# Hybrid encoder trunk: score products padded to 128 rows, and other prices in the planning clock

## The chip, the cores and the metric

The kernel runs on one core of a Trainium2 chip, in one launch. The metric is the device time of that launch in microseconds. TensorE (PE) multiplies, VectorE (DVE) and ScalarE (ACT) do the element-wise work, GpSimd (POOL) a few small operations, and SyncE (SP) issues the loads.

## The reference

Two layers of a block with four parallel branches, for 256 tokens of width 1024, all in float32. What matters here are the scores: per layer, two attentions and a retention of four heads of width 64 each.

```python
h = rms_norm(x, norm_mix_g)
rq, rk, rv, rg, pv, nq, nk, nv, mq = jnp.split(h @ w_in, 9, axis=-1)
...
sc = jnp.einsum('bhrnqd,bhrnwkd->bhrnqwk', qg, kg).astype(jnp.float32) * (d ** -0.5) + bias[None]
...
sc = jnp.einsum('bhsd,bhmd->bhsm', q, mk).astype(jnp.float32) * (q.shape[-1] ** -0.5)
...
scores = jnp.einsum('bhncd,bhnmd->bhncm', qc, kc) * d_intra[None, :, None].astype(dt)
...
x = x + merged @ w_out
a, g = jnp.split(rms_norm(x, norm_ffn_g) @ w_ffn_in, 2, axis=-1)
return x + (jax.nn.silu(a) * g) @ w_ffn_out
```

## The kernel before

The tokens form two tiles of 128 (tile 0, tile 1). The weights pass as slots of [128, 1024] in a fixed order: SyncE loads a slot into one of four `raw` buffers, ScalarE rounds it into one of ten `whi` buffers, VectorE makes the rest `wlo = raw - whi`. The left operands are split in the same way (`hhi`, `hlo` for the normalised activations, `bhi`, `blo` for the branches and the FFN's hidden part), and each product of 128 x 512 is three products: hi by hi, hi by lo, lo by hi. A slot gives six of them for each tile. The results gather in the PSUM banks `A` (two for each tile) and `B`; the banks `C` take transposes and what the branches need.

The order of all queues is written at build time by a planner. `Clock` holds an estimate of when each engine gets to what it was given: `Engine` passes on every call and enters it with a price from `Clock.cost`, `Clock.enter` adds waits for operands. The main loop emits a slot of products for one tile, and between groups of three products `background` lets go on those chains of small work (norms, heads, attention, gates, the FFN's hidden part) whose operands should be there by this clock, and `pump` hands out splits of weights. So a price changes no result, and shifts where small work stands between the products.

The scores of a head are made by `scores`. `to_heads` lays out `LS`: for head parity i, hi of the 64 rows of the head on its own partitions, and lo on the other 64. `RS` has hi of the right side on both halves, `RL` lo of it on the head's own 64. So the first product (`rs,ls`, 128 rows) gives hi by hi plus lo by hi, and the second (`rl,ls`, 64 rows) hi by lo. An attention calls it four times in a row, for two heads and both tiles, in two rounds; the retention calls it twice for each head. `log_sigmoid` makes the logarithms of the decays once, in layer 0, in scratch tiles of its own; `rgb` is a gain that is loaded later.

The names in the rows: `A<-whi,hhi` is a product of a rounded slot with a rounded activation, `C<-ident_gain,w` a transpose of a head's or the hidden part's tile `w`, `mem<-in_pool_a` the load of the pooling matrices into the buffers that held the memory tokens. L59 is the line that passes on every recorded call, so nearly all rows have it.

Of the kernel before, what the change touches and what calls it, by code (L numbers as in the profile page):

```python
# [9 lines left out]
F32 = mybir.dt.float32  # L10
# [25 lines left out]
WARM = 6.6  # L36
WINDOW = (6, 4, 1.5, 0.4)
# [5 lines left out]
class Engine:  # L43
    """An engine of nc whose instructions are also entered in the clock."""
# [4 lines left out]
    def __getattr__(self, op):  # L49
        f = getattr(self.real, op)  # L50

        def call(*args, **kw):
            outs = [kw[k] for k in ("out", "accum_out") if kw.get(k) is not None]
            ins = [v for k, v in kw.items() if k not in ("out", "accum_out")]
            rest = list(args)
            if "out" not in kw:
                outs.append(rest.pop(0))
            self.clock.enter(self.name, op, outs, [v for v in ins + rest if isinstance(v, bass.AP)], kw)
            return f(*args, **kw)  # L59

        return call


class Clock:
    """An estimate in microseconds of when each engine gets to what has been given to it:
    the small work is handed out when its operands should be there, so that no queue waits on it."""
# [3 lines left out]
    def __init__(self):  # L70
        self.at = dict.fromkeys(("PE", "ACT", "DVE", "POOL", "SP", "DMA"), 0.6)
        self.reads, self.writes = {}, {}
        self.mark = 0.0
        self.column = None

# [4 lines left out]
    def cost(self, eng, op, outs, ins, kw):  # L80
        n = max([x.free_size() for x in outs[-1:] + ins[:1]])
        if eng == "PE":
            o = outs[0]
            n = o.free_size() * (2 if self.now < WARM else 1)
            if op == "transpose":
                return n * 0.84e-3
            if ins[0].dtype == F32R:
                return n * 0.416e-3 + 0.003
            half = o.partition_size() == HD and o.base_partition()
            if o.partition_size() == HD:  # L90
                pair, self.column = self.column, None if half else n
                if half and pair == n:
                    return 0.02
            return max(n, 128) * 1.67e-3
        if eng == "ACT":
            return 0.1 + n * 0.83e-3 + 0.1 * (kw.get("accum_out") is not None) + 0.04 * isinstance(kw.get("scale"), bass.AP)
        if eng == "POOL":
            return 0.3 + 0.17 * n
        if op in ("tensor_copy", "tensor_scalar", "tensor_scalar_mul", "tensor_scalar_add", "memset"):
            return 0.07 + n * 0.55e-3  # L100
        return 0.07 + n * 1.05e-3 + 0.05 * (op == "scalar_tensor_tensor")
# [18 lines left out]
    def enter(self, eng, op, outs, ins, kw):  # L120
        ins = [x for x in ins if x.space != bass.MemoryType.DRAM]
        outs = [x for x in outs if x.space != bass.MemoryType.DRAM]
        skip = "PE" if eng == "PE" else None
        t = max([self.last(self.writes, x) + self.LATENCY for x in ins]
                + [self.last(self.reads, x, eng) + self.LATENCY for x in ins if x.space == bass.MemoryType.PSUM]
                + [max(self.last(self.writes, x, skip), self.last(self.reads, x, skip)) + self.LATENCY for x in outs] + [self.at[eng]])
        if op == "dma_start":
            self.at[eng] = t + 0.48
            t = max(self.at["DMA"], t + 1.1) + (outs + ins)[0].nbytes() / 360e3
            self.at["DMA"] = t  # L130
            end = t + 0.9
        else:
            end = self.at[eng] = t + self.cost(eng, op, outs, ins, kw)
        for x in ins:
            self.note(self.reads, x, end, eng)
        for x in outs:
            self.note(self.writes, x, end, eng)
        self.mark = max(self.mark, end)
# [9 lines left out]
def tile_encoder(ctx: ExitStack, tc: tile.TileContext, a: dict, out: bass.AP):  # L148
# [29 lines left out]
    RL = st([P, 2, S], F32R, "rl")  # L178
# [108 lines left out]
    def pump():  # L287
        """split weights when the engines have caught up, the sooner the fewer slots are ready"""
        window = WINDOW[max(0, min(state["lo"] - items[min(pos[0], len(items) - 1)]["j"], len(WINDOW) - 1))]
        if state["urgent"]:  # L290
            window = min(window, 0.8)
        for _ in range(2):
            j = state["lo"]
            if j < state["hi"] and soon(clock.at["DVE"], window) and soon(clock.last(clock.writes, WHI[j % NS])):
                split_lo()
            j = state["hi"]
            if (j < min(n_slots, state["free"] + NS, state["lo"] + NR) and soon(clock.at["ACT"], window)
                    and soon(clock.last(clock.writes, RAW[j % NR]))
                    and soon(max(clock.last(clock.reads, w[j % NS]) for w in (WHI, WLO)))):
                split_hi()  # L300
# [31 lines left out]
    def start(gen, *reads):  # L332
        """reads: PSUM banks that gen still reads, until it calls done()"""
        hold(*reads)
        chains.append([clock.now, gen])

    def until(step):
        """a chain goes on after what it has just given out (None), that much later (a number), or at a time"""
        return step[0] if isinstance(step, tuple) else clock.mark + (step or 0)

    def background():
        """let every chain go on whose last instructions should be through"""
# [39 lines left out]
    def scale_rows(out, in_, col):  # L382
        """out = in_ * col, on the engine that is free sooner"""
# [6 lines left out]
    def hi_lo(hi, lo, ps, bank, flag):  # L390
        """hi now, lo when hi is there, which ends the hold on bank"""
# [14 lines left out]
    def half_norm(src, t, c, act, gain, flag, bank, pre=None):  # L406
        """Half c of src (token-major) transposed, times gain (there a column), and split.
        What follows the products with it scales by one over the RMS (rms_chain)."""
# [22 lines left out]
    def rms_chain(src, rs, junk, flag, after=()):  # L431
        """rs = one over the RMS of each row of src"""
# [11 lines left out]
    def norm(t, flag, gain, rs, pre):  # L444
        """both halves of the norm of X[t]"""
# [7 lines left out]
    def head_norm(ps, dst, g, scale=None):  # L453
        """dst = ps (times scale, by row) scaled to unit RMS in groups of 64, g of them."""
# [78 lines left out]
    def to_heads(left, right, gains):  # L533
        """Token-major [tok, 256], both, to heads with the token in the free dimension, split for scores left^T right:
        LS has hi of a head on its 64 partitions and lo on the others, RS hi on both, and RL lo."""
# [31 lines left out]
        for i in range(2):  # L567
            lo(RL[own[i]], C[1], gains[1], i, RS[own[i], i])
# [3 lines left out]
    def scores(out, h, tok):  # L572
        """the scores of head h, for the tokens tok of left, with all of right"""
        r, i = h // 2, h % 2
        own = slice(i * HD, (i + 1) * HD)
        nc.tensor.matmul(out, LS[:, i, r, tok], RS[:, i, r, :], start=True, stop=False)
        nc.tensor.matmul(out, LS[own, i, r, tok], RL[own, r, :], start=False, stop=True)

    def attention(l, v, branch, bias):
        """softmax(q k + bias) v for four heads, two at a time, to BHI/BLO[branch]."""  # L580
# [122 lines left out]
    def decay_chain(l):  # L703
        """exp(|i - j| log gamma): the lesser of d lg_fwd and -d lg_bwd, both of which are at most 0 on their side"""
# [17 lines left out]
    def prefetch_chain(l):  # L722
        """parameters, and what comes in once the layer's norms are through"""
# [33 lines left out]
    def log_sigmoid():  # L757
        """lg = log sigmoid of the 16 decays: min(x, 0) - log1p(exp(-|x|))."""
        t0, t1, t2 = (st([P, 16], F32, f"ls{i}") for i in range(3))
# [26 lines left out]
    def add(n_js, act, bank, nk, n=512, first=True, last=True, req=None, end=None, lag=1):  # L786
        """bank(t) (+)= act of tile t @ the weights of the next n_js slots; nk k-tiles.
        req: what has to be there; end(t): what follows; lag: slots by which tile 0 may lead here."""
# [53 lines left out]
    def hid_chain(l, j, t, ps):  # L842
        """silu(a) * g, token-major"""
# [25 lines left out]
    def layer(l):  # L869
# [23 lines left out]
        for n, br in enumerate(BRANCHES):  # L893
            for blk in range(2):
# [3 lines left out]
                # the gates of the first branch lie around the memory's product  # L898
# [49 lines left out]
    def ready(t):  # L948
        """when the next slot of tile t can be taken"""
# [34 lines left out]
    def warm(*aps):  # L984
        """products of zeros, which keep TensorE at its full clock until aps are there"""
# [9 lines left out]
    with tc.manual_schedule():  # L995
        nc.vector.memset(W[0][:, 0:P], 0.0)
        nc.vector.memset(mhalf, -0.5)
        def load_x(t, c):
# [118 lines left out]
```

## Time and profile before

| | us |
|---|---|
| three runs | 849.38, 851.39, 854.74 |
| their median | 851.39 |
| the profiled execution, span from first to last instruction | 850.4 |
| TensorE busy in it | 840.0 |
| VectorE busy | 553.3 |
| ScalarE busy | 469.6 |

The profiled execution has its span alone; no other time is recorded around it, and the span lies between the fastest and the slowest run. TensorE's granted clock is 0.998 of full speed over the span. Products overlap: each row of a product has a start and a duration, and what a product costs is read from the start of one to the start of the next. An engine's row with [us <-releaser] stood idle that long before it.

### The profile page before, as it was taken

What the parts mean: (1) busy time and instruction counts of PE and PEld (TensorE: products, weight loads), DVE (VectorE), ACT (ScalarE), POOL (GpSimd) and SP (SyncE); (2) the same over time, 40 slices, a digit from 0 to 9 for tenths busy, and PEclk for the clock granted to TensorE, in tenths of its full rate; (3) what the DMA queues carried; (4) which work ended last, traced back from release to release, by engine and by line L of the source; (5) the groups of instructions that cost most, each with busy time, mean ns of one, the idle gap of its engine ahead of it and who ended that gap; (6) DMA issues with size and microseconds to landing.
All of it is one profiled execution on the core that took longest, in us unless ns stands there. A gap on an engine that the chain in (4) does not pass through costs nothing.

```text
span 850.4 us, 10796 instructions
## 1 busy us (share of the span) xinstructions
PE 840.0 (99%) x3934; PEld 678.6 (80%) x3934; DVE 553.3 (65%) x807; ACT 469.6 (55%) x722; POOL 28.6 (3%) x30
## 2 busy tenths in 40 slices
PE   8999999999999999999999999999999999999998
PEld 7887777778887888888888877777788878888886
DVE  5898776665667656555568778567665775665541
ACT  7867867444556444444469676664454654444430
POOL 0300100000000000000012001000000000000000
PEclk9999999999999999999999999999999999999999
DMA  8946764454558666665363567345554675656611
GB/s 267 315 131 202 246 201 132 131 191 160 191 169 259 188 196 187 186 188 186 96 218 121 173 216 250 134 124 182 165 170 131 190 252 183 190 181 192 193 53 50
DMA packets 103749, 152.86 MB, mean 180 GB/s; under 512 B 6416, under 2 KB 55312, under 8 KB 103696
## 3 DMA queue, kind: packets, MB, share of 16 engines
q1 hardware_dynamic: 103696, 152.17, 56.3%
q8 instruction: 31, 0.51, 0.2%
q14 instruction: 22, 0.18, 0.1%
HBM read 151.10 MB, written 1.05 MB: 179 GB/s over the span
## 4 chain that ended last, share of the span: by engine, by line
PE 94%; DMA 3%; DVE 1%; ACT 1%; SPq 0%; issue 0%; DVEq 0%; ACTq 0%
PE A L59 62%; PE B L59 27%; PE C L59 5%; DMA raw<-in_w_ffn_out 2%; DMA mem<-in_pool_a 1%; DVE wlo L59 1%; DMA x<-in_x 1%; ACT whi L59 1%; DVE w L59 0%; SPq L59 0%; DVE x L59 0%; DVEq L1113 0%; ACTq L59 0%
## 5 line engine op out<-in xcount | busy, mean ns | idle before, releaser
L59 DVE TENSOR_TENSOR wlo<-raw,whi 128x1024 fp32r<-128x1024 f32 (+1 forms) x275 | 329.9, 1211 | 183.6 <-ACT whi L59 182.7
L59 ACT CAST whi<-raw 128x1024 fp32r<-128x1024 f32 x272 | 284.3, 1051 | 221.2 <-PE A L59 102.1
L59 PE MATMUL A<-whi,hhi 128*128 128x512 f32 (+1 forms) x544 | 215.6, 396 | 0.1
L59 PE MATMUL A<-whi,hlo 128*128 128x512 f32 (+1 forms) x544 | 209.4, 385 | 0.0
L59 PE MATMUL A<-wlo,hhi 128*128 128x512 f32 (+1 forms) x544 | 209.0, 384 | 0.0
L59 PEld LDWEIGHTS A<-whi,hhi 128*128 128x128 f32 x544 | 102.4, 188 | 24.1 <-issue 5.5
L59 PEld LDWEIGHTS A<-whi,hlo 128*128 128x128 f32 x544 | 102.4, 188 | 21.2 <-DVE hlo L59 0.5
L59 PEld LDWEIGHTS A<-wlo,hhi 128*128 128x128 f32 x544 | 102.6, 189 | 17.9
L59 PE MATMUL B<-whi,hlo 128*128 128x512 f32 x288 | 112.3, 390 | 0.1
L59 PE MATMUL B<-whi,hhi 128*128 128x512 f32 x288 | 112.3, 390 | 0.0
L59 PE MATMUL B<-wlo,hhi 128*128 128x512 f32 x288 | 112.1, 389 | 0.0
L59 PE MATMUL A<-whi,bhi 128*128 128x512 f32 x272 | 109.2, 401 | 0.0
L59 PE MATMUL A<-whi,blo 128*128 128x512 f32 x272 | 106.3, 391 | 0.0
L59 PE MATMUL A<-wlo,bhi 128*128 128x512 f32 x272 | 106.1, 390 | 0.0
L59 PEld LDWEIGHTS B<-whi,hlo 128*128 128x128 f32 x288 | 54.0, 188 | 12.1 <-DVE hlo L59 0.9
L59 PEld LDWEIGHTS B<-wlo,hhi 128*128 128x128 f32 x288 | 54.1, 188 | 11.2
L59 PEld LDWEIGHTS B<-whi,hhi 128*128 128x128 f32 x288 | 54.1, 188 | 11.1
L59 PEld LDWEIGHTS A<-whi,bhi 128*128 128x128 f32 x272 | 51.1, 188 | 11.4 <-issue 0.8
L59 PEld LDWEIGHTS A<-whi,blo 128*128 128x128 f32 x272 | 51.0, 188 | 11.0
L59 PEld LDWEIGHTS A<-wlo,bhi 128*128 128x128 f32 x272 | 51.2, 188 | 9.7
L59 DVE SCALAR_TENSOR_TENSOR w<-B,rms,w 128x256 f32<-128x256 f32 x72 | 34.6, 482 | 3.9 <-ACT w L59 2.6
L59 ACT CAST bhi<-C 128x512 fp32r<-128x512 f32 x28 | 16.4, 587 | 35.2 <-PE C L59 35.1
(112 smaller groups left out, 614.9 us busy)
## 6 DMA issues: line engine op xcount, KB each, us to landing
raw<-in_w_ffn_in SPq DMA_DIRECT2D x176, 256.0 KB, 3.3
raw<-in_w_gate SPq DMA_DIRECT2D x64, 512.0 KB, 3.8
raw<-in_w_ffn_out SPq DMA_DIRECT2D x44, 512.0 KB, 4.0
raw<-in_w_in SPq DMA_DIRECT2D x36, 512.0 KB, 4.6
raw<-in_w_branch SPq DMA_DIRECT2D x16, 512.0 KB, 5.0
raw<-in_w_out SPq DMA_DIRECT2D x16, 512.0 KB, 4.1
raw<-in_w_mem_kv SPq DMA_DIRECT2D x8, 512.0 KB, 5.1
xn<-in_bias SPq DMA_DIRECT2D x4, 512.0 KB, 5.8
```

The lines of the kernel that those rows point to most:

```text
L59: return f(*args, **kw)
```

## The change

`RL` gets a place for each head parity, as `RS` has, with zeros on the 64 partitions that are not the head's own; the zeros are written once, by two memsets of GpSimd ahead of everything else, and `to_heads` writes only the head's own half. The second product of `scores` then runs over all 128 rows with the whole of `LS`, whose other half meets zeros. `log_sigmoid` takes its scratch from the still empty `rgb` instead of tiles of its own. In the clock, prices change: a product of 512 columns 0.216 to 0.227 us, transposes, VectorE's rows and DMAs a little, products of 64 output partitions get 0.2 at each change of width, memsets on GpSimd their own price, and a change between Exp and Sigmoid on ScalarE is entered with 1.28.

```diff
+TABLE_LOAD = 1.28
...
-            self.clock.enter(self.name, op, outs, [v for v in ins + rest if isinstance(v, bass.AP)], kw)
+            func = next((v for v in rest if isinstance(v, AF)), None)
+            self.clock.enter(self.name, op, outs, [v for v in ins + rest if isinstance(v, bass.AP)], kw, func)
...
+            narrow = op == "matmul" and ins[0].dtype == F32 and o.partition_size() == HD
+            change = 0.2 * (narrow != self.narrow)
+            self.narrow = narrow
             if op == "transpose":
-                return n * 0.84e-3
+                return n * 0.845e-3 + change
             if ins[0].dtype == F32R:
-                return n * 0.416e-3 + 0.003
+                return n * 0.4167e-3 + 0.0135 + change
...
-            return max(n, 128) * 1.67e-3
+            return max(n, 128) * 1.67e-3 + change
...
         if eng == "POOL":
+            if op == "memset":
+                return 0.1 + n * 1e-3
             return 0.3 + 0.17 * n
         if op in ("tensor_copy", "tensor_scalar", "tensor_scalar_mul", "tensor_scalar_add", "memset"):
-            return 0.07 + n * 0.55e-3
-        return 0.07 + n * 1.05e-3 + 0.05 * (op == "scalar_tensor_tensor")
+            return 0.085 + n * 0.6e-3
+        return 0.08 + n * 1.045e-3 + 0.05 * (op == "scalar_tensor_tensor")
...
+        if func in (AF.Exp, AF.Sigmoid) and func != self.table:
+            self.table = func
+            self.at["ACT"] += TABLE_LOAD
+            t = max(t, self.at["ACT"])
         if op == "dma_start":
-            self.at[eng] = t + 0.48
-            t = max(self.at["DMA"], t + 1.1) + (outs + ins)[0].nbytes() / 360e3
+            self.at[eng] = t + 0.45
+            t = max(self.at["DMA"], t + 1.2) + (outs + ins)[0].nbytes() / 390e3
             self.at["DMA"] = t
-            end = t + 0.9
+            end = t + 1.0
...
-    RL = st([P, 2, S], F32R, "rl")
+    RL = st([P, 2, 2, S], F32R, "rl")
...
-            lo(RL[own[i]], C[1], gains[1], i, RS[own[i], i])
+            lo(RL[own[i], i], C[1], gains[1], i, RS[own[i], i])
...
     def scores(out, h, tok):
         r, i = h // 2, h % 2
-        own = slice(i * HD, (i + 1) * HD)
         nc.tensor.matmul(out, LS[:, i, r, tok], RS[:, i, r, :], start=True, stop=False)
-        nc.tensor.matmul(out, LS[own, i, r, tok], RL[own, r, :], start=False, stop=True)
+        nc.tensor.matmul(out, LS[:, i, r, tok], RL[:, i, r, :], start=False, stop=True)
...
-        t0, t1, t2 = (st([P, 16], F32, f"ls{i}") for i in range(3))
+        t0, t1, t2 = (rgb[:, 16 * i:16 * i + 16] for i in range(3))
...
         nc.vector.memset(mhalf, -0.5)
+        for i in range(2):
+            nc.gpsimd.memset(RL[(1 - i) * HD:(2 - i) * HD, i].bitcast(F32), 0.0)
```

The number of products stays the same on TensorE; their order changes at many places. Three of them follow. In the order lists the numbers behind names tell buffers apart (`whi_73` to `whi_82` are the ten in turn, `wlo_83` to `wlo_92` their rests, `A_61`, `A_62` tile 0's banks, `A_63`, `A_64` tile 1's).

VectorE at the start of the program, before: `hlo_95` and `hlo_96` are the rests of the first norm's pieces for tile 0 and tile 1, `wlo_83` to `wlo_85` those of slots 0 to 2.

```order
L59 SCALAR_TENSOR_TENSOR hlo_95<-C_67,ident_gain,hhi_93 128x128 x4
L59 TENSOR_TENSOR wlo_83<-raw_69,whi_73 128x512 x2
L59 SCALAR_TENSOR_TENSOR hlo_96<-C_68,ident_gain,hhi_94 128x128 x4
L59 TENSOR_TENSOR wlo_84<-raw_70,whi_74 128x512 x2
L59 SCALAR_TENSOR_TENSOR hlo_95<-B_66,ident_gain,hhi_93 128x128 x4
L59 SCALAR_TENSOR_TENSOR hlo_96<-A_64,ident_gain,hhi_94 128x128 x4
L59 TENSOR_TENSOR wlo_85<-raw_71,whi_75 128x512 x2
```

The same place of VectorE's queue now:

```order
L61 SCALAR_TENSOR_TENSOR hlo_95<-C_67,ident_gain,hhi_93 128x128 x4
L61 TENSOR_TENSOR wlo_83<-raw_69,whi_73 128x512 x2
L61 SCALAR_TENSOR_TENSOR hlo_96<-C_68,ident_gain,hhi_94 128x128 x4
L61 SCALAR_TENSOR_TENSOR hlo_95<-B_66,ident_gain,hhi_93 128x128 x4
L61 SCALAR_TENSOR_TENSOR hlo_96<-A_64,ident_gain,hhi_94 128x128 x4
L61 TENSOR_TENSOR wlo_84<-raw_70,whi_74 128x512 x2
L61 TENSOR_TENSOR wlo_85<-raw_71,whi_75 128x512 x2
```

`wlo_84` moved behind the second pieces of both tiles. TensorE's rows there changed too: the four transposes into `A_64` stand directly behind those into `B_66`, and slot 0 is taken for both tiles (three and six products) before slot 1 for tile 0.

TensorE at the transposes of the second FFN block's hidden part (`w_127` of tile 0, `w_128` of tile 1) in layer 0, before:

```order
L59 MATMUL A_62<-whi_82,hhi_93 128x512
L59 MATMUL A_62<-wlo_92,hhi_93 128x512
L59 MATMUL A_62<-whi_82,hlo_95 128x512
L59 MATMUL A_62<-whi_82,hhi_93 128x512
L59 MATMUL A_62<-wlo_92,hhi_93 128x512
L59 MATMUL A_62<-whi_82,hlo_95 128x512
L59 MATMUL C_68<-ident_gain,w_127 128x128
L59 MATMUL C_68<-ident_gain,w_128 128x128
L59 MATMUL C_68<-ident_gain,w_127 128x128
L59 MATMUL C_68<-ident_gain,w_128 128x128
```

The same place of TensorE's queue now:

```order
L61 MATMUL A_62<-whi_82,hhi_93 128x512
L61 MATMUL A_62<-wlo_92,hhi_93 128x512
L61 MATMUL A_62<-whi_82,hlo_95 128x512
L61 MATMUL C_68<-ident_gain,w_127 128x128
L61 MATMUL C_68<-ident_gain,w_128 128x128
L61 MATMUL C_68<-ident_gain,w_127 128x128
L61 MATMUL C_68<-ident_gain,w_128 128x128
L61 MATMUL A_62<-whi_82,hhi_93 128x512
L61 MATMUL A_62<-wlo_92,hhi_93 128x512
L61 MATMUL A_62<-whi_82,hlo_95 128x512
```

The four transposes moved ahead of the slot's last three products; layer 1 has the same move.

SyncE's queue around the load of the pooling matrices in layer 0, before:

```order
L59 DMA raw_70<-in_w_gate 128x2x512
L59 DMA raw_71<-in_w_gate 128x2x512
L59 DMA raw_72<-in_w_gate 128x2x512
L59 DMA mem_123<-in_pool_a 128x1024
L59 DMA mem_124<-in_pool_a 128x1024
L59 DMA raw_69<-in_w_branch 128x2x512
```

The same place of SyncE's queue now:

```order
L61 DMA raw_70<-in_w_gate 128x2x512
L61 DMA raw_71<-in_w_gate 128x2x512
L61 DMA mem_123<-in_pool_a 128x1024
L61 DMA mem_124<-in_pool_a 128x1024
L61 DMA raw_72<-in_w_gate 128x2x512
L61 DMA raw_69<-in_w_branch 128x2x512
```

The two loads moved ahead of one weight slot. On TensorE the last transposes before them moved by twelve products, and the pooling products that read the matrices follow those transposes after 18 products instead of 21.

## Rows read from the trace of the kernel before

**Rows 1.** The page: the span, and TensorE's busy time, share and instructions.

```profile
span 850.4 us, 10796 instructions
PE 840.0 (99%) x3934; PEld 678.6 (80%) x3934; DVE 553.3 (65%) x807; ACT 469.6 (55%) x722; POOL 28.6 (3%) x30
```

**Rows 2.** Waits of TensorE: us in total, times, longest.

```profile
PE C L59 <- DVE w L59: 2.8, 4, 1.1
```

**Rows 3.** Timeline of TensorE, 107.3 to 110.7 us: start, duration, what.

```profile
107.44 0.39 PE L59 MATMUL A<-whi,blo 128*128 128x512 f32 x1
107.67 0.28 PE L59 MATMUL B<-rs,ls 128*128 128x256 f32 x1
107.87 0.38 PE L59 MATMUL B<-rl,ls 64*128 64x256 f32 x1
108.18 0.38 PE L59 MATMUL B<-rs,ls 128*128 128x256 f32 x1
...
110.06 0.50 PE L59 MATMUL A<-whi,bhi 128*128 128x512 f32 x1
110.40 0.40 PE L59 MATMUL A<-wlo,bhi 128*128 128x512 f32 x1
```

**Rows 4.** Groups by shape: count, busy us, mean ns, idle before.

```profile
L59 PE MATMUL B<-rl,ls 64*128 64x256 f32 x48 | 18.3, 381 | 0.0
L59 PE MATMUL B<-rs,ls 128*128 128x256 f32 x48 | 16.7, 349 | 0.0
L59 PEld LDWEIGHTS B<-rs,ls 128*128 128x128 f32 x48 | 9.0, 187 | 4.8
L59 PE MATMUL A<-whi,hlo 128*128 128x256 f32 x32 | 9.1, 283 | 0.0
```

**Rows 5.** Timeline of TensorE in the pooling projection, from 65.7 us.

```profile
65.80 0.28 PE L59 MATMUL A<-whi,hlo 128*128 128x256 f32 x1
65.92 0.28 PE L59 MATMUL A<-whi,hhi 128*128 128x256 f32 x1
```

**Rows 6.** Timeline of TensorE and VectorE at the start.

```profile
10.85 0.75 PE L59 MATMUL B<-ident_gain,x 128*128 128x128 f32 x4
...
11.17 1.28 DVE L59 TENSOR_TENSOR wlo<-raw,whi 128x512 fp32r<-128x512 f32 x2
...
13.94 1.13 DVE L59 SCALAR_TENSOR_TENSOR hlo<-A,ident_gain,hhi 128x128 fp32r<-128x128 f32 x4
...
14.99 1.28 DVE L59 TENSOR_TENSOR wlo<-raw,whi 128x512 fp32r<-128x512 f32 x2
```

**Rows 7.** Timeline of TensorE at the second FFN block's transposes, layer 0.

```profile
267.77 0.27 PE L59 MATMUL C<-ident_gain,w 128*128 128x128 f32 x1
...
269.10 0.55 PE L59 MATMUL C<-ident_gain,w 128*128 128x128 f32 x3 [1.05 <-DVE w L59]
```

**Rows 8.** Timeline of TensorE at the FFN norm of tile 1, layer 0.

```profile
249.04 1.04 PE L59 MATMUL C<-ident_gain,x 128*128 128x128 f32 x8
...
250.85 0.39 PE L59 MATMUL B<-wlo,hhi 128*128 128x512 f32 x1
251.26 0.50 PE L59 MATMUL B<-whi,hlo 128*128 128x512 f32 x1
```

**Rows 9.** The chain that ended last, layer 1: the pooling matrices.

```profile
591.34 6.72 DMA mem<-in_pool_a
...
598.10 0.78 PE B L59 x12
```

**Rows 10.** Timeline from the first heads' transposes to the first scores.

```profile
35.56 1.03 PE L59 MATMUL C<-ident_gain,w 128*128 128x128 f32 x8
...
44.21 1.53 DVE L59 SCALAR_TENSOR_TENSOR rl<-C,cols,rs 64x512 fp32r<-64x512 f32 x2
...
46.01 0.38 PE L59 MATMUL B<-rl,ls 64*128 64x256 f32 x1
```

**Rows 11.** Busy time of each engine from 14 to 64 us.

```profile
14.00:64.00 50.00, 50.00 (x246) 41.43 (x245) 44.04 (x94) 38.76 (x78) 9.26 (x8) 1.00 0.68 225
```

More of the change, by code (lines that the diff above doesn't have):

```diff
@@ L74, in __init__ @@
         self.column = None
+        self.narrow = False
+        self.table = None
     @property
@@ L118, in note, with enter @@
         table[key] = old + [(p0, p1, lo, hi, end, eng)]
-    def enter(self, eng, op, outs, ins, kw):
+    def enter(self, eng, op, outs, ins, kw, func=None):
         ins = [x for x in ins if x.space != bass.MemoryType.DRAM]
```

## The prediction

> **What bounds the kernel now.** I read the page first, then the waits, then the timeline of TensorE. The page says that TensorE is busy for 840.0 of 850.4 us, and VectorE for much less [rows 1]; the list of waits says how little TensorE stands still behind another engine once the start is over, 2.8 us in four waits for VectorE [rows 2]. So the sequence of products is the time: an edit pays what it takes out of TensorE's own queue, and a new order of the small work can win back only that 2.8 us and the short waits under the list's threshold, while it can lose at each place where TensorE now arrives a little earlier than the small work does. The timeline shows what is slow in the queue itself. Where the score products run, starts lie far apart although nothing is waited for [rows 3].
>
> **Padding the score products.** A head's scores are two products, `rs,ls` over 128 rows and `rl,ls` over 64; 48 of each run in a pass [rows 4]. In the block of eight at 107.67 us the first change of height costs 0.20 us from start to start and each later one 0.31; the block lasts from 107.67 to 110.06, and the product behind it takes 0.34 us to the next start where an ordinary one takes 0.23 [rows 3]: 2.39 + 0.11 = 2.50 us. The attentions have eight such blocks (two branches, two halves, two layers): 20.0 us. Retention has eight blocks of four; one such is 2.50 - 4 x 0.313 = 1.25 us, so 10.0 us. Together 30.0 us.
>
> After the edit both products have 128 rows and 256 columns. No score product of that kind without a neighbour of another height stands in the trace; the nearest rows are the 256-column products of the pooling projection, also 128*128 with a weight load for each. They start every 0.12 us [rows 5], all 96 of them alike. 96 x 0.12 = 11.5 us, a saving of **18.5 us**, all on the path. The bounds: at best 0.12, since these columns must pass anyway; at worst the duration of a weight load, 0.187 us [rows 4], as the pace (18.0 us, saving 12.0). I take 0.12, because the pooling rows have the same shape, and a load of their own each.
>
> VectorE and ScalarE do the same amount of work for RL as before: the two lower halves are written into two places instead of one. The zeros come from two memsets of GpSimd, put ahead of everything; GpSimd's first task in the program is needed only after 16 us, and if they were to cost 1 us each this would hide them. The log-sigmoid scratch in `rgb` puts the load of `rgb` behind VectorE's last read of it, but its queue neighbour, a weight slot, waits for a later VectorE step anyway: nothing.
>
> **The new prices.** They change no instruction, only the order. The order lists show the following places where TensorE's operand is now nearer.
>
> (a) The start. VectorE makes slot 1's lower half (`wlo_84`) behind two more normalised pieces. Before, it ran at 11.17 us; those pieces end where the next step starts, at 14.99 [rows 6]. Half of such a split takes half of 1.28 us plus its tail, so the first half is there at 15.7. TensorE starts the B transposes at 10.85 [rows 6], then come eight transposes at 0.1 [rows 8], nine products at 0.23 and 0.1 for the restart, then the first product of slot 1: its second, which reads `wlo_84`, could start at 14.1. Wait **1.6 us**; nothing overtakes it in TensorE's queue, and the weight loads behind it (SyncE waits for the same step) have room until slot 5.
>
> (b) The second FFN block's transposes (`C_68<-w`). TensorE came at 267.77 us and waited to 269.10 [rows 7]. They now stand three products, 0.7 us, earlier, and ScalarE's and VectorE's rows ahead of their operand are the same: 0.7 us more in each layer, **1.4 us**.
>
> (c) The FFN norm of tile 0 now has three products between its eight transposes and the first product that reads them, as tile 1 has. Tile 1 pays for it: a start at 250.85 is followed by one at 251.26, 0.19 too late, and by a restart of 0.1 [rows 8]: 0.3 in each layer, **0.6 us**.
>
> (d) Pooling. The load of its matrices is issued one weight slot earlier, but the transposes move by the same, and the products that read it stand 18 instead of 21 products behind them. The second matrix landed at 598.06, and TensorE took it at 598.10, hardly waiting [rows 9]. Three products are 0.7 us in each layer; the first layer's may have slack. Between 0 and 1.4 us, I take **0.8**.
>
> (e) The first scores. Between the transposes of the heads (35.56) and the first `rl` product (46.01), which came 0.3 us behind VectorE's `rl` [rows 10], stood 42 products; now 27, 3.4 us less. VectorE has one weight split fewer in between (1.2 us, as [rows 6] has it for two halves with their tail), and its first operand is some 0.6 us earlier against the transposes. That leaves 1.3 us; if the weights ahead of `ls` on ScalarE land early, nothing. I take **0.7**.
>
> (f) The transposes for the heads of the memory branch are the other two of the four waits for VectorE [rows 2]. They stand twelve products later, but VectorE now puts two splits ahead of their last operand. Between -0.7 us, what two waits as long as that of (b) leave of the 2.8, and +1.2, half a split in each layer; I take 0.
>
> The FFN's steady part, half of the program, keeps its order: nothing.
>
> The sum: -18.5 + 1.6 + 1.4 + 0.6 + 0.8 + 0.7 = -13.4 us. From the span of 850.4, 837.0. The median of the runs shown, 851.4, lies 1.0 above that span, so I forecast **838 us**.
>
> **The rivals.** First, the padding does nothing. It assumes that the slow starts come from the change of height; they could come from weight loads that are not hidden. Then a score product costs its load and its columns, 0.187 + 0.12 = 0.31 us, about what is there now, the saving is nil and the new waits remain: 851.4 + 5 = 856. For it speaks that the sum fits; against it that the pooling products, each with its load, run at 0.12 [rows 5]. The Trainium skill's page "TensorE: Matmul & The Clock Gate" (Part 3, the mechanism) says that a weight load overlaps products in flight only when it goes to another group of rows; by that rule the padded products, all on the same rows, would give this time. The pooling rows disagree with it. 3%. A pace of 0.187 would give 851.4 - 12.0 + 5.1 = 844.5; 4%.
>
> Second, the prices do what they are for: (b) to (e) cost nothing and the 2.8 us of waits go too. 851.4 - 18.5 + 1.6 - 2.8 = 831.7 or less; 6% for below 831.
>
> Third, slower. VectorE is busy 44.0 of the 50 us from 14 to 64 [rows 11], and there the new order shifts most rows and issues the prefetched tables two weight slots earlier on SyncE. If the splits fall behind, TensorE waits for each slot. It decides against the kernel from 13.4 us of such waits upward, and 22 us make 860. VectorE's 6 idle us there must be used up first. 4%. Waits of 5 to 15 us more, of this or of other kinds, end within 1%: 5%.
>
> **How the numbers follow.** Forecast with its unknown terms: the low end takes the second rival's 831, the high end all upper bounds, 851.4 - 18.5 + 1.6 + 1.4 + 0.6 + 1.4 + 1.3 + 1.2 = 840.4, and 2.5 for the scatter of the runs, which lie 2.0 below to 3.3 above their median: 831 to 843, 78%. About 1% is what a measurement of this kernel can tell from no change, here 842.9. Faster 0.87 (forecast, second rival, and the edge of the others), the same 0.09, slower 0.04.
>
> **What would show it.** Right: `rl` products as 128*128, score starts 0.12 us apart, the product behind a block at 0.23. Each wait has its place: between 14 and 16 us behind VectorE's `wlo`, at the second FFN block's transposes 1.9 us instead of 1.3, before the pooling products, before the first scores. Wrong it would be by score starts above 0.15 us, or by waits of TensorE for `wlo` through the first 64 us.

## The result, and the profile after

The changed kernel takes 845.0 us (median of six runs, 842.6 to 847.8), the kernel before 850.9 (six runs): a ratio of 0.9925, 95% interval 0.9903 to 0.9946. Forecast were 838 us and a range of 831 to 843. Its profiled execution took 844.92 us, of which 843.0 are the span.

The page of the changed kernel, its first lines and the chain that ended last; they answer to [rows 1].

```profile
span 843.0 us, 10809 instructions
PE 825.2 (98%) x3936; PEld 673.7 (80%) x3936; DVE 553.0 (66%) x806; ACT 469.1 (56%) x723; POOL 30.3 (4%) x32
...
PE 79%; ACT 7%; DMA 6%; DVE 6%; issue 1%; POOL 1%; SPq 0%; DVEq 0%; ACTq 0%
```

TensorE's busy time fell by 14.8 us, the span by only 7.4: TensorE now stands still more. Only 79% of the chain is TensorE's own; before the change it was 94%:

```profile
PE 94%; DMA 3%; DVE 1%; ACT 1%; SPq 0%; issue 0%; DVEq 0%; ACTq 0%
```

The score products of one block, timeline of TensorE in the changed kernel (start, duration, what); before is in [rows 3].

```profile
112.69 0.40 PE L61 MATMUL A<-whi,blo 128*128 128x512 f32 x1
112.93 0.28 PE L61 MATMUL B<-rs,ls 128*128 128x256 f32 x1
113.04 0.27 PE L61 MATMUL B<-rl,ls 128*128 128x256 f32 x1
113.15 0.28 PE L61 MATMUL B<-rs,ls 128*128 128x256 f32 x1
...
113.86 0.40 PE L61 MATMUL A<-whi,bhi 128*128 128x512 f32 x1
114.10 0.40 PE L61 MATMUL A<-wlo,bhi 128*128 128x512 f32 x1
```

Eight score products take 113.86 - 112.93 = 0.93 us, 0.12 each, and the product behind them 0.24 instead of 0.34. That is the forecast pace.

TensorE's waits in the changed kernel (engine and tile, what it waited for: us in total, times, longest); before is in [rows 2].

```profile
PE C L61 <- DVE w L61: 5.0, 4, 1.5
PE C L61 <- DMA x<-in_x: 2.3, 1, 2.3
PE A L61 <- DVE wlo L61: 1.8, 2, 1.3
PE C L61 <- DVE ls L61: 1.3, 1, 1.3
PE B L61 <- DVE mhalf L61: 1.0, 1, 1.0
PE C L61 <- DVE blo L61: 1.0, 2, 0.9
PE A L61 <- ACT gt L61: 0.5, 1, 0.5
PE C L61 <- ACT pt L61: 0.4, 1, 0.4
PE B L61 <- DMA mem<-in_pool_a: 0.2, 1, 0.2
```

The waits for `x` and `mhalf` belong to the start, before and after. The wait for `w` rose from 2.8 to 5.0 us, and six kinds are new. Where they stand (without the short ones of 0.2 us), timeline of TensorE (a row with brackets stood idle that long, for what the arrow names):

```profile
14.12 0.39 PE L61 MATMUL A<-whi,hhi 128*128 128x512 f32 x1
15.78 0.50 PE L61 MATMUL A<-wlo,hhi 128*128 128x512 f32 x1 [1.27 <-DVE wlo L61]
16.12 0.39 PE L61 MATMUL A<-whi,hlo 128*128 128x512 f32 x1
...
34.40 0.66 PE L61 MATMUL C<-ident_gain,mem 128*128 128x128 f32 x4 [0.87 <-DVE blo L61]
...
44.78 0.44 PE L61 MATMUL C<-ident_gain,mem 128*128 128x128 f32 x2 [1.29 <-DVE ls L61]
...
105.65 0.52 PE L61 MATMUL C<-ident_gain,w 128*128 128x128 f32 x3 [0.95 <-DVE w L61]
...
112.12 0.50 PE L61 MATMUL A<-whi,bhi 128*128 128x512 f32 x1 [0.49 <-ACT gt L61]
...
264.28 0.27 PE L61 MATMUL C<-ident_gain,w 128*128 128x128 f32 x1
265.94 0.55 PE L61 MATMUL C<-ident_gain,w 128*128 128x128 f32 x3 [1.39 <-DVE w L61]
...
473.54 0.50 PE L61 MATMUL A<-wlo,hhi 128*128 128x512 f32 x1 [0.52 <-DVE wlo L61]
...
501.40 1.08 PE L61 MATMUL C<-pt,qk 128*64 128x256 f32 x6 [0.41 <-ACT pt L61]
...
516.01 0.52 PE L61 MATMUL C<-ident_gain,w 128*128 128x128 f32 x3 [1.17 <-DVE w L61]
...
679.88 0.55 PE L61 MATMUL C<-ident_gain,w 128*128 128x128 f32 x3 [1.49 <-DVE w L61]
```

From start to start a wait costs a little more than the brackets say: 15.78 - 14.12 = 1.66 where 0.23 is usual, and the next start, at 16.12, is 0.1 late as well. The sequence of waits is longer than the forecast's: the two for bank C at 34 and 45 us, the gate at 112, `wlo` at 473 and `pt` at 501 us were not in it.

### The profile page after: what moved, and what is told of

Same layout as the page of the kernel before. It is cut to its first block, busy times and chain, and to the rows that moved or that the text cites. A ratio compares the mean times of both kernels' runs of the same rounds, so it can differ in the third digit from the quotient of the medians.

```text
span 843.0 us, 10809 instructions
## 1 busy us (share of the span) xinstructions
PE 825.2 (98%) x3936; PEld 673.7 (80%) x3936; DVE 553.0 (66%) x806; ACT 469.1 (56%) x723; POOL 30.3 (4%) x32
## 3 DMA queue, kind: packets, MB, share of 16 engines
HBM read 151.10 MB, written 1.05 MB: 180 GB/s over the span
## 4 chain that ended last, share of the span: by engine, by line
PE 79%; ACT 7%; DMA 6%; DVE 6%; issue 1%; POOL 1%; SPq 0%; DVEq 0%; ACTq 0%
PE A L61 50%; PE B L61 25%; PE C L61 4%; DVE wlo L61 3%; ACT whi L61 2%; DMA raw<-in_w_ffn_out 2%; DMA raw<-in_w_gate 1%; DVE w L61 1%; DMA raw<-in_w_in 1%; ACT sc L61 1%; DMA mem<-in_pool_a 1%; ACT L61 1%; DMA x<-in_x 1%; ACT qk L61 1%; POOL sm L61 1%
```

## Experiments: padding and order apart

Theory: the padding is worth its 18.5 us in any order, and the order that the new prices write costs some 11 us. Rival: a shorter queue of TensorE meets the same small work sooner, whatever the order.

**pad_only**: the changed kernel with the old prices. TensorE's and SyncE's queues have the order of before, row for row.

```diff
-TABLE_LOAD = 1.28
+TABLE_LOAD = 0.0
...
-                return n * 0.4167e-3 + 0.0135 + change
+                return n * 0.416e-3 + 0.003
```

The other prices of the clock are as before too; the memsets keep their own.

> The padded scores with every price of the clock as it was before (the two memsets are priced apart, so that TensorE's queue has the order of before, row for row). Order theory: padding is worth its full 18.5 us under any order, and the order made by the new prices is what costs about 11 us in waits of TensorE; so 851 - 18.5 = 832.5 us (830 to 835), and the waits behind VectorE stay near the 2.8 us of before. Exposure theory: a TensorE queue that is 18.5 us shorter meets the same small work earlier, and waits for it whatever the order; so 842 to 846 us, as the changed kernel, with PE's waits of 10 us or more.

**prices_only**: the new prices with score products of 64 rows; TensorE's queue has the order of the changed kernel.

```diff
-        nc.tensor.matmul(out, LS[:, i, r, tok], RL[:, i, r, :], start=False, stop=True)
+        own = slice(i * HD, (i + 1) * HD)
+        nc.tensor.matmul(out, LS[own, i, r, tok], RL[own, i, r, :], start=False, stop=True)
```

> The new prices with score products of 64 rows as before; TensorE's queue has the order of the changed kernel, row for row. Order theory: 845 + 18.5 = 863.5 us (859 to 865), slower than before by about 11 us. Exposure theory: the new order costs nothing by itself, 849 to 853 us, within 1% of before.

| | old order | new order | the order costs |
|---|---|---|---|
| 64-row scores | 850.9 | 859.9 | 9.0 |
| 128-row scores | 834.3 | 845.0 | 10.7 |
| the padding saves | 16.6 | 14.9 | |

pad_only has a ratio of 0.980 (0.9787 to 0.9813), prices_only of 1.0099 (1.0084 to 1.0115). So the order by itself costs 9.0 and 10.7 us, within 2 us of the theory's 11. The padding saves 1.9 and 3.6 us less than the theory's 18.5; what the rival names, an earlier meeting with the same small work, can have at most those. Waits of TensorE in pad_only:

```profile
PE C L61 <- DMA x<-in_x: 2.4, 1, 2.4
PE C L61 <- DVE w L61: 2.1, 3, 1.0
PE B L61 <- DVE mhalf L61: 1.0, 1, 1.0
PE B L61 <- DMA mem<-in_pool_a: 0.3, 1, 0.3
PE B L61 <- DVE rl L61: 0.3, 1, 0.3
```

They are the waits of before and two short ones, for the pooling matrices and for `rl`. The spans say the same: 850.4, 833.3 with the padding (-17.1), 843.0 with the new order too (+9.7).

## Experiments: which price

Two kernels divide the new prices into TensorE's and the others.

**pe_old**: the changed kernel, TensorE's prices put back.

> The changed kernel with TensorE's prices alone put back (products of 512 columns at 0.216 us, no price for a change of width), all other new prices kept. If the price of TensorE's products carries the waits (the old one, 5% too fast, made the clock put small work later among the products than it needed, which was slack), 832 to 836 us. If the other prices carry them (table loads, VectorE, loads from memory), 843 to 847 us.

**not_pe**: the changed kernel, TensorE's new prices kept, those of VectorE, the loads and the table change put back.

> The changed kernel with the prices of VectorE, of the loads and of the table change put back, and TensorE's new prices kept. If TensorE's price carries the waits, 843 to 847 us or a little more (small work is also thought faster than it is); if the others carry them, 832 to 836 us.

Measured: pe_old 842.2 us (840.0 to 843.6), not_pe 850.3 (847.9 to 852.5). Neither is near 832 to 836 us, so neither group carries the loss by itself: against 834.3, TensorE's prices alone cost 16.0 us, the others alone 7.9, both together 10.7. So I went on from pad_only with single changes, among them two that put no price right.

**pad_prod** (0.227 instead of 0.216 us for a product of 512 columns), **pad_table** (`TABLE_LOAD = 1.28`), **pad_lat13** and **pad_lat10** (the clock's wait between engines, each one line), all else as in pad_only:

```diff
-    LATENCY = 0.12
+    LATENCY = 0.13
```

> The padded kernel with all old prices but one: a product of 512 columns costs 0.227 us in the clock instead of 0.216. Slack theory (the old price, 5% under what the trace shows, left room between small work and the products that read it; the right price takes that room away): 842 to 850 us, as TensorE's prices together gave 850.3. Draw theory (any change of a price writes another order, and the order of before is one of the better ones): 836 to 845 us, no nearer to 850 than other changes. If the price of a change of width made the 850.3, about 834 us.

> The padded kernel with all old prices but the table change, entered at 1.28 us on ScalarE, which is what the trace shows for one (1283 ns). Slack theory: small work is thought later, so TensorE meets it later: no cost, 832 to 835 us. Draw theory: 837 us or more.

> The padded kernel with all old prices, and the clock's wait between engines 0.13 instead of 0.12 us: a nudge that puts no price right and takes no slack away. Slack theory: 832 to 835 us, as pad_only's 834.3. Draw theory: another order is another time, 837 us or more.

> The padded kernel with all old prices, and the clock's wait between engines 0.10 instead of 0.12 us; 154 lines of difference in TensorE's order list, where 0.13 us made 362. Draw theory: another order is another time, 836 us or more; if the loss goes with the rows that move, about 838 us. If only later small work costs, not earlier, 834 us.

**after_lat30**: the changed kernel with `LATENCY = 0.30`.

> The changed kernel, all new prices, with the clock's wait between engines 0.30 instead of 0.12 us, so that all small work is thought later than the new prices alone say. Slack theory: the room is back and the waits at the heads, the gates and the FFN's transposes go, 833 to 839 us. Draw theory: one more order, anywhere from 836 to 850 us.

| the padded kernel with | us | above pad_only |
|---|---|---|
| LATENCY 0.10 | 837.6 | 3.3 |
| table change | 838.3 | 4.0 |
| all new prices, LATENCY 0.30 | 841.5 | 7.2 |
| the others' new prices (pe_old) | 842.2 | 7.9 |
| LATENCY 0.13 | 843.3 | 9.0 |
| all new prices | 845.0 | 10.7 |
| product price | 845.6 | 11.3 |
| TensorE's new prices (not_pe) | 850.3 | 16.0 |

The kernels were timed in several sets, and the median of the kernel before lay between 850.9 and 851.9 us in them: a difference of 1 us between rows says nothing.

The slack theory falls: a hundredth of a microsecond, which takes no room away, costs 9.0 us, and later small work (pad_table) costs too. 0.30 us gives 3.5 of the 10.7 back. The draw theory holds: eight new orders of the same padded kernel, eight losses, 3.3 to 16.0 us. They follow the size of the move only loosely: the table change moves more rows of TensorE's queue than LATENCY 0.13 and costs less than half of it, and LATENCY 0.30 moves the most. TensorE waits in each of them, at other places each time; pad_lat13's longest, among TensorE's waits:

```profile
PE C L61 <- ACT pt L61: 2.2, 1, 2.2
PE B L61 <- ACT sc L61: 2.1, 1, 2.1
```

Waits are not the whole loss. In the profiled executions of seven of the eight, all but the changed kernel, a stretch at half the granted clock stands at such waits or right behind them; before, pad_only, pad_ffn_later and after_wlo_ffn show none after the start. Two of them, in windows (us, busy time of PE, PEld, DVE, ACT, POOL, granted clock, DMA share, GB/s) of pad_prod and of after_lat30:

```profile
102.40:106.60 4.20, 4.20 (x14) 3.41 (x15) 3.79 (x5) 3.86 (x6) 0.00 (x0) 0.62 0.66 208
```

```profile
554.00:558.50 4.50, 4.50 (x14) 3.70 (x13) 2.07 (x3) 3.48 (x6) 0.00 (x0) 0.50 0.16 62
```

In pad_prod's 4.20 us at 0.62, TensorE does what takes 2.6 us at full clock: 1.6 us are lost without a wait. How much of each loss is clock is open, as not every execution of a kernel need have such a stretch: pad_lat10's profiled one had a mean granted clock of 0.998, its other three had 1.000 and were 0.4 to 0.7 us shorter.

## Experiments: single waits mended

Here no price changes. A few instructions move, and every other row of every queue stays.

**after_wlo_early**: in the changed kernel, slot 1's rest is issued ahead of the second normalised pieces, as before; the clock is told of it where the changed kernel has it.

```diff
...
         done(bank)
+        if flag == "h1@0" and c == 0:
+            for o in HALVES:
+                tc.nc.vector.tensor_sub(WLO[1][:, o], RAW[1][:, o], WHI[1][:, o].bitcast(F32))
         state["urgent"] -= urgent
```

> The changed kernel, with one thing moved on VectorE alone: the two halves of slot 1's rest (wlo_84) ahead of the second normalised pieces again, as before; every other row of every queue is the changed kernel's. Chain theory: the late wlo_84 also holds its raw buffer, so the next loads start late, VectorE and ScalarE are about 1.1 us behind from 21 us on, and the waits for bank C at 33 and 43 us follow from it. Then the waits at 14, 33 and 43 us (1.4, 1.0, 1.4) go together: 845.0 - 3.9 = 841.1 us. If each wait stands for itself, only the one at 14 us goes: 843.5 us. If the start is bound by its loads anyway, TensorE waits for something else there: 845 us.

**after_wlo_ffn**: that, and the second FFN block's transposes three products later. **pad_ffn_later**: the same line in pad_only, where it moves them by six.

```diff
     def hid_T(l, j):
         yield from need(f"hid{j}0@{l}", f"hid{j}1@{l}")
-        yield
+        yield 1.4 if j == 1 else None
```

> The one above, and the four transposes of the second FFN block three products later in both layers, as before the change; nothing else moves. If waits are what their length says, 0.7 us less per layer than the one above: 1.4 us less in all. If what follows the transposes is late then too, the gain is given back behind them: the same time as the one above.

> The padded kernel with the old prices, and the second FFN block's transposes six products (1.4 us) later in both layers; no other row moves. Its trace shows waits of 0.2 and 1.2 us there. They should go, with a tenth for the restart of each: 834.3 - 1.5 = 832.8 us; 834 if the waits are given back behind the transposes.

after_wlo_early: 841.7 us (838.3 to 847.2), ratio 0.9873 (0.9845 to 0.9901). after_wlo_ffn: 839.3 (838.5 to 839.5), 0.9844 (0.9827 to 0.9861). pad_ffn_later: 832.2 (831.0 to 834.0), 0.9764 (0.9745 to 0.9783); it beats both kernels. Against pad_only that is 2.2 us less by the medians of two sets of runs, and 1.1 by the two profiled spans (833.3 and 832.2).

The start, in a window of the changed kernel (columns as in the windows of pad_prod):

```profile
14.00:18.00 4.00, 2.73 (x13) 1.90 (x12) 3.97 (x12) 3.94 (x9) 0.00 (x1) 1.00 0.16 23
```

The same window of after_wlo_ffn:

```profile
14.00:18.00 4.00, 4.00 (x20) 3.30 (x19) 3.43 (x9) 3.94 (x9) 0.55 (x1) 1.00 0.99 358
```

In the changed kernel almost nothing is loaded from 14 to 18 us, 23 GB/s: `raw_70` is held by the late split, and the loads queue behind it. With the split early they run at 358. The waits at 14 and 34 us are gone, the one at 45 shrinks, and a new one of 0.31 us stands at 20 us (timeline of TensorE in after_wlo_ffn):

```profile
20.68 0.50 PE L61 MATMUL A<-wlo,hhi 128*128 128x512 f32 x1 [0.31 <-DVE wlo L61]
...
42.46 0.66 PE L61 MATMUL C<-ident_gain,mem 128*128 128x128 f32 x4 [0.83 <-DVE ls L61]
...
261.80 0.27 PE L61 MATMUL C<-ident_gain,w 128*128 128x128 f32 x1
262.74 0.44 PE L61 MATMUL C<-ident_gain,w 128*128 128x128 f32 x2 [0.67 <-DVE w L61]
```

So the chain theory holds in part: the wait at 34 us hung on the start, that at 45 only for a third. after_wlo_early's median fell by 3.3 us with a wide scatter. Its profiled execution was the longest of its six and has a half-clock stretch too (granted clock 0.50 from 588 to 591 us), so the rows are those of after_wlo_ffn, which has the same start. The FFN transposes waited 262.74 - 261.80 = 0.94 us instead of 1.66, 0.72 less for three products' delay: in layer 0 that wait is as long as TensorE is early. What follows takes nothing back: the lead over the changed kernel is 265.94 - 262.74 = 3.20 us there and 473.54 - 469.60 = 3.94 us in layer 1. In pad_only the same block waited in layer 1, and in pad_ffn_later neither layer's does (timelines of TensorE: pad_only in layer 1, then pad_ffn_later in layer 0; in layer 1 no wait stands there either):

```profile
669.55 0.27 PE L61 MATMUL C<-ident_gain,w 128*128 128x128 f32 x1
670.87 0.55 PE L61 MATMUL C<-ident_gain,w 128*128 128x128 f32 x3 [1.05 <-DVE w L61]
```

```profile
262.27 0.60 PE L61 MATMUL C<-ident_gain,w 128*128 128x128 f32 x4
262.62 0.48 PE L61 MATMUL A<-whi,hhi 128*128 128x512 f32 x1
```

## Why the prediction was wrong

The sum, in spans: forecast 837.0, measured 843.0. Of the 6.0 us, 1.4 are the padding (17.1 saved instead of 18.5) and 4.6 the new order (9.7 instead of 5.1). Another 0.9 is the step from span to time: I added 1.0, from a median of runs beside one span; in the changed kernel the profiled execution itself shows 1.9.

**The step that failed is the sum of the new order's waits, (a) to (f):** 5.1 us forecast, 9.7 measured. Its mechanism was right, TensorE arriving before small work, and its size was not. I priced the places where the lists show an operand nearer, and set everything else at nothing without a reason; some 4 us of waits stand there.

- Padding: right. The pace is 0.12, a block's follower 0.24. Of the 1.4 us that it lost, 0.8 stand in one block of pad_only, where TensorE, sooner at the scores, waits for `rl`: from 105.21 to 106.99 us, 1.78 instead of 0.95. Where the rest went is open.
- First rival, padding does nothing: wrong. The padded products have a weight load of 188 ns each, all on 128 rows, and start every 0.12 us. The rule of the Trainium skill's page "TensorE: Matmul & The Clock Gate" (Part 3, the mechanism), that a load overlaps only with products on other rows, does not describe these rows. The same section also says that a load into the background weight buffer is pulled ahead; no run here shows which buffer a load goes to.
- (a) 1.6 forecast, 1.4 and 0.1 for the restart measured, at the place forecast. What I wrote behind it, that the loads have room until slot 5, was wrong: they stood for the rest of 14 to 18 us. after_wlo_early shows that the wait at 34 us and part of that at 45 hang on it.
- (b) 1.4 forecast; after_wlo_ffn, which undoes this move, gives 0.72 back in layer 0, and in layer 1 the wait's bracket falls from 1.49 to 0.54. Right.
- (c) 0.6 forecast, and the timeline has it at tile 0: starts at 230.50, 230.89 and 231.23 us, 0.16 and 0.11 late, and the same in layer 1 at 644.74. Right. (d) 0.8 forecast; the list of waits shows 0.2 for `pool_a`, where pad_only has 0.3 without the new order. (e) 0.7 forecast for the first scores: no wait there. What that stretch lost, it lost earlier, at the memory transposes that need bank C. So 1.5 us of (d) and (e) did not come; by luck they hid a part of what was left out.
- (f) I took 0 from a range of -0.7 to 1.2. The waits at the memory branch's heads are 0.95 and 1.17 in the changed kernel. In pad_only the list's 2.1 us for `w`, less 1.05 at the FFN in layer 1, leave 1.05 for the two. So 1.1 us were added: the upper end was the right one.
- Not in the sum: the bank C waits at 34 and 45 us, the gate at 112, `wlo` at 473, `pt` at 501. In the brackets 0.87 + 1.29 + 0.49 + 0.52 + 0.41 = 3.6 us, with 0.1 for each restart 4.1. What then still lacks of the 9.7 is not found.
- "The FFN's steady part keeps its order: nothing": right, no wait stands between 270 and 430 us.
- Second rival, prices mend waits: wrong way round. The product's new price, 0.227, is what the trace shows: in the changed kernel's chain (start, us, what) 147 products take 33.56 us, 0.228 each. Yet this price alone costs 11.3 us.

```profile
175.10 33.56 PE A L61 x147
```

- Third rival, VectorE behind from 14 to 64 us: the place was right, the size not. TensorE there, in the changed kernel (a row of windows):

```profile
14.00:64.00 50.00, 46.57 (x223) 37.89 (x222) 43.89 (x97) 35.84 (x74) 11.16 (x8) 1.00 0.64 215
```

It was busy for all 50.0 us before [rows 11], and now for 46.57: 3.4 us of the loss lie in this stretch. VectorE is no busier than before, 43.89 us to 44.04, and had not used up its 6 idle us first, as this rival wanted: moving one of its splits forward takes two of the waits away (after_wlo_ffn).

Shown are that the order costs, that undoing two of its moves gave back about the length of the waits there, and that no one price does it. Only argued is why the order of before is better than eight others: its prices may have been picked by the time they gave. The waits at the heads, the gate, `wlo` at 473 and `pt` were not undone one by one, so some 5 us between after_wlo_ffn and pad_only (4.2 in spans) rest on the trace alone, and its list of waits names about half of them.

## What to carry to other kernels

Where a cost table writes the order, a price is no description but a draw: time the table alone and the other edit alone before joining them. Count a re-ordered program at the loss that a meaningless nudge of the table gives (in this kernel 3 to 9 us), not at the waits that can be seen in its lists. A wait that the trace names is better mended by moving its own few instructions than by prices: in pad_ffn_later that kept every other row in place and paid 1 to 2 us.

## What the runs showed of the hardware

Two things stand out. Where score products of 64 and 128 rows alternate, each start is 0.19 us later, though no engine waits: 0.31 from start to start [rows 3], and 0.12 when all have 128. That it is the change of height, and not the 64 rows themselves, fits the starts of both kinds being 0.31 apart; no row has score products of 64 rows side by side, so it is not shown.

And a wait of TensorE can cost more than its length. In pad_lat10 it stood 2.4 us; the products behind it started 0.23 us apart for a microsecond, then 0.43 apart for 3.4 us. The granted clock is 0.64 over the window, a mixture of full and half clock, 2.4 and 1.2 GHz (timeline, and the window's row):

```profile
100.38 0.52 PE L61 MATMUL C<-ident_gain,w 128*128 128x128 f32 x3 [2.40 <-DVE w L61]
...
101.43 0.42 PE L61 MATMUL A<-whi,hhi 128*128 128x512 f32 x1
101.66 0.62 PE L61 MATMUL A<-wlo,hhi 128*128 128x512 f32 x1
102.07 0.63 PE L61 MATMUL A<-whi,hlo 128*128 128x512 f32 x1
...
105.06 0.40 PE L61 MATMUL A<-whi,hhi 128*128 128x512 f32 x1
```

```profile
100.40:105.00 4.60, 4.60 (x15) 3.72 (x16) 4.54 (x5) 4.49 (x8) 0.00 (x0) 0.64 0.82 250
```

Eight products at 0.2 us more are 1.6 us on top of the wait. The length of the wait alone does not settle whether such a stretch follows. In after_wlo_early the granted clock was 0.50 from 588 to 591 us behind a wait of 1.42 us; behind pad_lat13's 2.07 us it stayed at 1.00 from 500.5 to 507 us, and behind the changed kernel's waits, 1.5 us at the longest, there is no such stretch either.
